# Two transformer blocks in one kernel: the second block's modulations moved beside the first feed-forward, background work queued behind fixed instructions of VectorE, state-space tables cut into small steps

## The chip, the cores and the metric

The kernel runs on one core of one Trainium2 chip, as one launch. The metric is the device time of a launch in microseconds; before the change it is 2636.41 us, the median of three runs (2634.53, 2636.41 and 2639.88).

## What is computed

512 tokens of width 1024 go through two blocks; 256 context tokens go with them through the first half of block 1. Cut to what matters here:

```
# block 1 (x: 512 tokens, h: 256 context tokens; c, c_ctx: one vector each)
ml = silu(c) @ ada_w + ada_b          # 9 vectors of 1024: shifts, scales, gates
mc = silu(c_ctx) @ ada_w + ada_b      # the first 5 of them are used
x = x + 0.5*ml[2] * swiglu(rms(x)*(1+ml[1])+ml[0])     # ffn1, x and h
h = h + 0.5*mc[2] * swiglu(rms(h)*(1+mc[1])+mc[0])
x = x + ml[5] * token_mix(...)                          # mLSTM and HGRN scans
x = x + 0.5*ml[8] * swiglu(rms(x)*(1+ml[7])+ml[6])      # ffn2
x = rms(x)                                              # final norm
# block 2
sh1, sc1, gt1, sh2, sc2, gt2 = split(silu(c_2) @ w_ada + b_ada, 6)
x = x + gt1 * mix(rms(x)*(1+sc1)+sh1)                   # attention and S5 state-space mixer
x = x + gt2 * conv_swiglu(rms(x)*(1+sc2)+sh2)           # up, causal conv, down
```

The S5 mixer needs tables (powers of a complex decay times its input and output matrices, a rotation table and a short kernel) that depend on weights alone.

## The kernel before, in words

**Matmuls.** Activations lie with features on partitions and tokens on the free axis. Each float32 weight tile (128x1024) is loaded into `wraw` (L195), copied into a rounded half `whi` by ScalarE (L203), and VectorE writes the rest `wlo` (L204); `mm3` (L208 to L218) makes a product of three passes, `whi*xh` (L215), `whi*xl` (L216) and `wlo*xh` (L218). There are three buffers of each.

**A feed-forward** (`ffn`, L424) has 11 groups. `stage_in` makes two hidden tiles of a group: PSUM tiles `psa` and `psu` (and `psc` for the context tokens), SiLU on ScalarE, a product `sa` (L438) and its split `hh`, `hl` (L441, L442). `stage_out` of the group before adds the down projection: eight tiles `pso`, from two banks, which VectorE adds to the residual `xr` (L491) or, for the context, `hr` (L494). The first hidden tile of a feed-forward is done in two halves of 256 tokens (L464 to L468), as its input is normalised half by half: `ssq_rstd` (L367) squares and sums the residual, takes a root on ScalarE (L374), a reciprocal on VectorE (`col`, L375), and spreads the result over partitions by four matmuls (L363) into `rs`; `norm_tile` then makes eight tiles `nt`, `xmh`, `xml` (L401 to L408) by VectorE, ScalarE and GpSimd.

**Modulations.** Those of ffn1's own input are made ahead of it (`ffn1_start`). The others come from `ada_steps` (L286): the rows of the modulation matrix come in tiles of 1 MB (`araw`, L293, two buffers, SyncE's queue), and VectorE multiplies each of their two halves with the broadcast vector `crow` (its SiLU is L283) and sums, by one SCALAR_TENSOR_TENSOR with an accumulator each (L305). Block 1 has 28 such tiles and 80 accumulations, and they are the background of ffn1. Block 2 has 24 tiles and 48 accumulations, and they are the background of ffn2, ahead of the S5 tables (`s5_tables`, L1383 on): some 200 short VectorE instructions, twelve GpSimd ones of 2048 columns (`big4`, L1509), 40 transposes and 64 small matmuls.

**Order.** The background is a Python generator. `tick()` (L322) runs it to its next `yield`, and is called twice after each hidden tile and once after every four output tiles. A tick decides only where instructions stand in the program text: a list scheduler then orders each engine's queue by that place and by when it takes an operand to be ready, so background work that is ready early is issued early. What the background still has to do is emitted before group 10 (`drain`).

Of the kernel before, what the change touches and what calls it, by code (L numbers as in the profile page):

```python
# [8 lines left out]
F32 = mybir.dt.float32  # L9
# [5 lines left out]
ALU = mybir.AluOpType  # L15
# [127 lines left out]
class Net:  # L143
# [142 lines left out]
    def ada_steps(self, src, bias, ids, jobs, done=None):  # L286


        nc = self.nc
        cr = self.c_rows(ids)  # L290
        todo = [(c, b0 + b, b, outs) for c, b0, outs in jobs for b in range(4)]

        def load(i):  # L293
            if i < len(todo):
                w = self.adp.tile([128, 2, D], F32, tag="araw", name=self.nm("araw"), bufs=2)
                nc.sync.dma_start(w, src[todo[i][1]])
                return w
        w = load(0)
        for i, (c, _, b, outs) in enumerate(todo):
            nxt = load(i + 1)  # L300
            for n, o in enumerate(outs):
                for h in range(2):
                    k = 2 * b + h
                    junk = self.adp.tile([128, D], BF16, tag="ajunk", name=self.nm("ajunk"), bufs=1)
                    nc.vector.scalar_tensor_tensor(junk, w[:, h], 1.0, cr[:, n], ALU.mult, ALU.mult,  # L305
                                                   accum_out=o[:, k : k + 1])
                yield
            if b == 3:
                for o in outs:
# [9 lines left out]
        yield  # L319
        self.tc.cur_priority -= n  # L320

    def tick(self):  # L322
        if self.bg is not None:
            next(self.bg, None)

    def drain(self):
        for _ in self.bg or ():
# [96 lines left out]
    def ffn(self, segs, w_in, w_out, act=None, group0=None, tail=None, nlast=2):  # L424
# [6 lines left out]
        def act_in(j, ps, hs):  # L431
            for si, (xm, wd, _, _) in enumerate(segs):
                if act is not None:
                    sa = act(ps[si][0], ps[si][1], j)
                else:
                    sa = self.tp.tile([128, T], F32, tag="sq", name=self.nm("sa"), bufs=4)[:, :wd]
                    nc.scalar.activation(sa, ps[si][0], AF.Silu)
                    nc.vector.tensor_tensor(sa, sa, ps[si][1], ALU.mult)  # L438
                hh = self.hhp.tile([128, wd], F32R, tag=f"hh{si}", name=self.nm("hh"), bufs=6)
                hl = self.hhp.tile([128, wd], F32R, tag=f"hl{si}", name=self.nm("hl"), bufs=6)  # L440
                nc.scalar.activation(hh, sa, AF.Copy)  # L441
                nc.vector.tensor_tensor(hl, sa, hh.bitcast(F32), ALU.subtract)  # L442
                hs[si].append((hh, hl))

        def stage_in(gi):
            hs = [[] for _ in segs]
            for jj, j in enumerate((gi * 2, gi * 2 + 1)):
                if gi == 0 and group0 is not None:
                    act_in(j, group0[jj], hs)
                    self.tick()  # L450
                    self.tick()
                    continue
                ww = [self.weights(w_in[2 * j + ai], [KT, 128]) for ai in range(2)]
                ws = [[(wh[:, k], wl[:, k]) for k in range(KT)] for wh, wl in ww]
# [17 lines left out]
                        for si, (xm, wd, _, _) in enumerate(segs):  # L472
                            self.mm3(ps[si][ai], ws[ai], xm)
                act_in(j, ps, hs)
                self.tick()
                self.tick()
            return hs

        def stage_out(gi, hs):
            ww = [self.weights(w_out[gi * 2 + jj], [D]) for jj in range(2)]  # L480
            w = lambda n: [(wh[:, n * 128 : n * 128 + 128], wl[:, n * 128 : n * 128 + 128]) for wh, wl in ww]
            for n2 in range(0, KT, 2):
                for si, (_, wd, res, gt) in enumerate(segs):
                    po = None
                    for n in (n2, n2 + 1):
                        if wd == T or n == n2:
                            po = self.bank("o", [128, 2, 256] if wd < T else [128, 512])
                        p = po if wd == T else po[:, n - n2]
                        self.mm3(p, w(n), hs[si])
                        if wd == T:  # L490
                            nc.vector.scalar_tensor_tensor(res[n], p, gt[:, n : n + 1], res[n], ALU.mult, ALU.add)  # L491
                    if wd < T:
                        for n in (n2, n2 + 1):
                            nc.vector.scalar_tensor_tensor(res[n], po[:, n - n2], gt[:, n : n + 1], res[n],  # L494
                                                           ALU.mult, ALU.add)
                if n2 % 4 == 2:
                    self.tick()

        def finish(gi, hs):

# [15 lines left out]
        for gi in range(NG):  # L516
            if gi == NG - 1:
                self.drain()
            hs.append(stage_in(gi))
            if gi == 1:  # L520
                self.tick()
                self.tick()
# [14 lines left out]
    def block1_ffn1(self):  # L537
        nc, tc = self.nc, self.tc
        with ExitStack() as es:
# [772 lines left out]
    def block1_ffn2(self):  # L1312
        nc, tc = self.nc, self.tc
        with ExitStack() as es:
            pool = lambda **k: es.enter_context(self.pool(**k))
            self.kinds = dict(u="a", s="p", o="t")
            self.tp, self.hhp = pool(name="tmp", bufs=2, side="right"), pool(name="hid", bufs=6)
            self.adp = self.bgs.enter_context(self.pool(name="ada", bufs=2, side="right"))
# [3 lines left out]
            jobs = [(c, 4 * c, (self.mod2[:, c],)) for c in range(6)]  # L1322
# [60 lines left out]
    def s5_tables(self, w, tag):  # L1383
# [19 lines left out]
        nc.scalar.activation(r8, mag, AF.Exp, scale=8.0)  # L1403
        nc.scalar.activation(mag, mag, AF.Exp)
        TT(th, li, step, mult)
        big = 1.5 * 2.0 ** 23
        nc.vector.tensor_scalar(n, th, 1.0 / (2 * np.pi), big, mult, add)
        nc.vector.tensor_scalar(n, n, big, None, sub)
        for c in (6.28125, 0.00193500518798828125, 3.0199159819567e-7):
            nc.vector.scalar_tensor_tensor(th, n, -c, th, mult, add)  # L1410
        lim = 3.1415925
        nc.vector.tensor_scalar(th, th, lim, -lim, ALU.min, ALU.max)
        u_re, u_im, ab = sm(), sm(), sm()
# [20 lines left out]
        at = lambda k: (P[0][:, :, k], P[1][:, :, k])  # L1434
        for k in range(2, 9):
            cmul(at(k), at(k // 2), at(k - k // 2))

        nre, den, fre, fim = sm(), sm(), sm(), sm()
        nc.vector.tensor_scalar(nre, P[0][:, :, 1], 1.0, None, sub)
# [5 lines left out]
        TT(t2, P[1][:, :, 1], li, mult)  # L1445
        TT(fre, t1, t2, add)
        TT(fre, fre, den, mult)
        TT(t1, P[1][:, :, 1], lr, mult)
        TT(t2, nre, li, mult)
        TT(fim, t1, t2, sub)  # L1450
# [12 lines left out]
        for o, (x, y), op in ((BB[0], (0, 1), sub), (BB[1], (1, 0), add)):  # L1463
            TT(o, bcw[:, x], c3(fre), mult)
            TT(tb, bcw[:, y], c3(fim), mult)
            TT(o, o, tb, op)

        U = [(u_re, u_im)]
        for _ in range(3):
            o = (sm(), sm())  # L1470
            cmul(o, U[-1], U[-1])
            U.append(o)
        rot = [sm((N, G, 64), tag="s5r") for _ in range(2)]
        nc.vector.memset(rot[0][:, :, 0], 1.0)
        nc.vector.memset(rot[1][:, :, 0], 0.0)
# [3 lines left out]
        while m < 64:  # L1479
# [4 lines left out]
            TT(hi[0], lo[0], b_[0], mult)  # L1484
            TT(t, lo[1], b_[1], mult)
            TT(hi[0], hi[0], t, sub)
            TT(hi[1], lo[0], b_[1], mult)
            TT(t, lo[1], b_[0], mult)
            TT(hi[1], hi[1], t, add)
            m *= 2  # L1490
            if m < 64:
                o = (sm(), sm())
                cmul(o, pw, pw)
                pw = o
        dt = lambda shape, nm: self.dp.tile(shape, F32, name=nm)
        self.s5d = dict(rot=dt([2, N, G, 64], "s5rot"), r8=dt([N, G], "s5r8"), bin=dt([2, N, G, N], "s5bin"),
                        out=dt([2, N, G, N], "s5out"), m=dt([N, 8, 512], "s5m"))
# [9 lines left out]
        yield  # L1507

        def big4(x, y, part, s0, s1):  # L1509
            o = w.tile([N, G, 8, 16], F32, tag="s5b", name=self.nm("s5b"), bufs=2)  # L1510
            t = w.tile([N, G, 8, 16], F32, tag="s5b", name=self.nm("s5b"), bufs=2)
            if part == 0:
                gp(o, x[0], y[0], mult)
                gp(t, x[1], y[1], mult)
                gp(o, o, t, s0)
            else:
                gp(o, x[0], y[1], mult)
                gp(t, x[1], y[0], mult)
                gp(o, o, t, s1)
            return o  # L1520
        krow, ksum = [sm((N, 8, N), tag="s5r") for _ in range(2)]
        for part in range(2):
            W1 = big4(pin, b4, part, sub, add)
            for q4 in range(4):
                pt = self.bank(tag, [N, 4, N])
                for x in range(4):
                    nc.tensor.transpose(pt[:, x], W1[:, q4 * 4 + x].rearrange("p t c -> p (t c)"), self.ident)
# [26 lines left out]
            if r < N:  # L1554
                nc.gpsimd.dma_start(self.s5d["m"][r:, t], zt[r:])
        for part in range(2):
            o = big4(pout, c4, part, add, sub)
# [511 lines left out]
```

## Time and profile before

| | |
|---|---|
| median of three runs | 2636.41 us |
| profiled execution, its time | 2634.42 us |
| its span, first to last instruction | 2632.6 us |
| TensorE matmuls busy | 2524.9 us, 96% |
| VectorE busy | 1653.0 us, 63% |
| ScalarE busy | 964.1 us, 37% |
| GpSimd busy | 458.8 us, 17% |
| mean granted TensorE clock | 0.977 |

The profile is of one execution, whose time is 1.8 us more than its span. A matmul that is issued late but overlaps the one before still counts as busy, so the 96% says less than the count of matmuls in a stretch does. In time the stages are: start to 80 us, ffn1 to some 570, the mix of block 1 to 1540, ffn2 to 1925, the mix of block 2 to some 2270, the last feed-forward to the end.

### The profile page before, as it was taken

What the parts mean: (1) busy time and instruction counts of PE and PEld (TensorE: products, weight loads), DVE (VectorE), ACT (ScalarE), POOL (GpSimd) and SP (SyncE); (2) the same over time, 40 slices, a digit from 0 to 9 for tenths busy, and PEclk for the clock granted to TensorE, in tenths of its full rate; (3) what the DMA queues carried; (4) which work ended last, traced back from release to release, by engine and by line L of the source; (5) the groups of instructions that cost most, each with busy time, mean ns of one, the idle gap of its engine ahead of it and who ended that gap; (6) DMA issues with size and microseconds to landing.
All of it is one profiled execution on the core that took longest, in us unless ns stands there. A gap on an engine that the chain in (4) does not pass through costs nothing. (4 is left out here: it accounts for less than half of the span.)

```text
span 2632.6 us, 38056 instructions
## 1 busy us (share of the span) xinstructions
PE 2524.9 (96%) x15116; PEld 2159.4 (82%) x15116; DVE 1653.0 (63%) x3071; ACT 964.1 (37%) x1710; POOL 458.8 (17%) x547
## 2 busy tenths in 40 slices
PE   6999999999989998999999988999999999999998
PEld 4888888899978888897888886788886768888887
DVE  8897534446499995425433489964565677766665
ACT  5311212236323332416422362222343466633333
POOL 3000000012044334314000012250012350100001
PEclk8999999999999999999999998999999899999999
DMA  6557211222211111111333376653414223333332
GB/s 228 178 193 252 91 55 57 81 72 79 71 49 41 49 33 41 37 56 50 103 111 92 118 228 224 218 179 98 151 41 147 57 64 102 120 96 96 96 96 73
DMA packets 88307, 277.94 MB, mean 106 GB/s; under 512 B 12912, under 2 KB 31104, under 8 KB 79936
## 3 DMA queue, kind: packets, MB, share of 16 engines
q1 hardware_dynamic: 85344, 265.00, 31.3%
q0 software_dynamic: 2064, 7.35, 0.8%
q10 hardware_dynamic: 720, 3.15, 0.3%
q8 instruction: 119, 1.95, 0.3%
q14 instruction: 60, 0.49, 0.1%
HBM read 262.88 MB, written 12.59 MB: 105 GB/s over the span
## 5 line engine op out<-in xcount | busy, mean ns | idle before, releaser
L204 DVE TENSOR_TENSOR wlo<-wraw,whi 128x1024 fp32r<-128x1024 f32 (+1 forms) x341 | 426.6, 1257 | 268.0 <-ACT whi L203 132.9
L203 ACT ACTIVATE whi<-wraw 128x1024 fp32r<-128x1024 f32 (+1 forms) x341 | 355.1, 1053 | 562.8 <-PE psp L216 157.2
L215 PE MATMUL psp<-xmh,whi 128*128 128x512 f32 (+1 forms) x760 | 283.6, 379 | 3.5 <-ACT K L807 3.1
L216 PE MATMUL psp<-xml,whi 128*128 128x512 f32 (+1 forms) x744 | 275.8, 377 | 0.0
L347 POOL TENSOR_TENSOR ssum<-ssum,sq 128x256 f32<-128x256 f32 x40 | 30.2, 755 | 1012.8 <-ACT sq L345 1012.4
L216 PE MATMUL psa<-xml,whi 128*128 128x512 f32 x496 | 194.7, 393 | 1.1 <-DVE xml L404 1.1
L215 PE MATMUL pso<-hh,whi 128*128 128x512 f32 (+1 forms) x512 | 185.7, 368 | 9.7 <-DVE xr L491 7.2
L215 PE MATMUL psa<-xmh,whi 128*128 128x512 f32 x496 | 194.9, 393 | 0.0
L216 PE MATMUL psu<-xml,whi 128*128 128x512 f32 x496 | 193.2, 390 | 0.0
L215 PE MATMUL psu<-xmh,whi 128*128 128x512 f32 x496 | 193.1, 389 | 0.0
L216 PE MATMUL pso<-hl,whi 128*128 128x512 f32 (+1 forms) x512 | 184.7, 366 | 0.0
L305 DVE SCALAR_TENSOR_TENSOR ajunk<-araw,crow 128x1024 bf16<-128x1024 f32 x128 | 160.6, 1254 | 25.9 <-DMA araw<-in_ada_r_dram 25.2
L215 PEld LDWEIGHTS psp<-xmh,whi 128*128 128x128 f32 x760 | 149.8, 197 | 28.8 <-ACT K L807 4.8
L218 PE MATMUL psp<-xmh,wlo 128*128 128x512 f32 (+1 forms) x744 | 172.2, 372 | 0.0
L216 PEld LDWEIGHTS psp<-xml,whi 128*128 128x128 f32 x744 | 146.8, 197 | 22.1 <-issue 0.6
L218 PEld LDWEIGHTS psp<-xmh,wlo 128*128 128x128 f32 x744 | 131.8, 193 | 26.3 <-issue 4.4
L218 PE MATMUL pso<-hh,wlo 128*128 128x512 f32 (+1 forms) x512 | 145.4, 365 | 3.4 <-DVE wlo L204 3.4
L491 DVE SCALAR_TENSOR_TENSOR xr<-pso,hgate,xr 128x512 f32<-128x512 f32 x128 | 94.9, 747 | 68.7 <-PE pso L218 68.6
L218 PE MATMUL psa<-xmh,wlo 128*128 128x512 f32 x496 | 126.4, 391 | 0.1
L218 PE MATMUL psu<-xmh,wlo 128*128 128x512 f32 x496 | 124.3, 390 | 1.3 <-DVE wlo L204 1.2
L441 ACT ACTIVATE hh<-sa 128x512 fp32r<-128x512 f32 x66 | 36.8, 562 | 241.9 <-DVE sa L438 241.7
L215 PEld LDWEIGHTS pso<-hh,whi 128*128 128x128 f32 x512 | 97.1, 190 | 27.3 <-DVE xr L491 5.8
(670 smaller groups left out, 5812.4 us busy)
## 6 DMA issues: line engine op xcount, KB each, us to landing
araw<-in_ada_r_dram SPq DMA_DIRECT2D x52, 1024.0 KB, 5.8
wraw<-in_ffn_in_dram SPq DMA_DIRECT2D x88, 512.0 KB, 3.9
wraw<-in_mix_fm_dram SPq DMA_DIRECT2D x65, 512.0 KB, 3.7
wraw<-in_ffn_out_dram SPq DMA_DIRECT2D x44, 512.0 KB, 3.7
wraw<-in_up_dram SPq DMA_DIRECT2D x44, 512.0 KB, 3.7
wraw<-in_down_dram SPq DMA_DIRECT2D x22, 512.0 KB, 3.7
araw<-in_ada_w_dram SPq DMA_DIRECT2D x8, 1024.0 KB, 11.8
wraw<-in_mix_out_dram SPq DMA_DIRECT2D x14, 512.0 KB, 3.7
```

What stands on the lines that cost most here:

```text
L203: nc.scalar.activation(hi, raw, AF.Copy)
L204: nc.vector.tensor_tensor(lo, raw, hi.bitcast(F32), ALU.subtract)
L215: self.nc.tensor.matmul(ps, wh, xh, start=k == 0, stop=False)
L216: self.nc.tensor.matmul(ps, *((wl, xh) if last else (wh, xl)), start=False, stop=False)
L218: self.nc.tensor.matmul(ps, *((wh, xl) if last else (wl, xh)), start=False, stop=k == n - 1)
L305: nc.vector.scalar_tensor_tensor(junk, w[:, h], 1.0, cr[:, n], ALU.mult, ALU.mult, accum_out=o[:, k : k + 1])
L347: (eng or nc.vector).tensor_tensor(acc, acc, t, ALU.add)
L441: nc.scalar.activation(hh, sa, AF.Copy)
L491: nc.vector.scalar_tensor_tensor(res[n], p, gt[:, n : n + 1], res[n], ALU.mult, ALU.add)
```

## The change

1. All 52 modulation tiles are now the background of ffn1, block 1's first and then block 2's; ffn2 keeps the S5 tables alone. The generator yields after every accumulation instead of after every two.
2. `tick(n)` runs the generator `n` times, inside `issue_after(anchor)`: every VectorE instruction that it emits gets an edge, for order in the queue only, behind the anchor. The anchor is the last `hl` of a hidden tile or the last residual addition of a `stage_out`. Ticks run 4 steps after a hidden tile and 3 after four output tiles in ffn1, and 2 and 1 in ffn2.
3. `s5_tables` yields after each short group of instructions. `big4` becomes `quarter`, called 16 times: of its three instructions, each now on 512 columns, the second product moves from GpSimd to VectorE.

```diff
@@ ada_steps
                     nc.vector.scalar_tensor_tensor(junk, w[:, h], 1.0, cr[:, n], ALU.mult, ALU.mult,
                                                    accum_out=o[:, k : k + 1])
-                yield
+                    yield
@@
-    def tick(self):
+    def tick(self, n=1):
         if self.bg is not None:
-            next(self.bg, None)
+            with self.tc.issue_after(self.anchor.ins):
+                for _ in range(n):
+                    next(self.bg, None)
@@ act_in
-                nc.vector.tensor_tensor(hl, sa, hh.bitcast(F32), ALU.subtract)
+                self.anchor = nc.vector.tensor_tensor(hl, sa, hh.bitcast(F32), ALU.subtract)
@@ stage_in
-                self.tick()
-                self.tick()
+                self.tick(self.pace[0])
@@ stage_out
-                            nc.vector.scalar_tensor_tensor(res[n], p, gt[:, n : n + 1], res[n], ALU.mult, ALU.add)
+                            self.anchor = nc.vector.scalar_tensor_tensor(res[n], p, gt[:, n : n + 1], res[n],
+                                                                         ALU.mult, ALU.add)
...
                 if n2 % 4 == 2:
-                    self.tick()
+                    self.tick(self.pace[1])
@@ block1_ffn1
-            self.bg = self.ada_steps(self.ins["ada_r"], "ada_b", (0, 1), jobs, done)
+            jobs2 = [(c, 4 * c, (self.mod2[:, c],)) for c in range(6)]
+
+            def bg():
+                yield from self.ada_steps(self.ins["ada_r"], "ada_b", (0, 1), jobs, done)
+                yield from self.ada_steps(self.ins["ada_r2"], "ada_b2", (2,), jobs2)
+            self.bg, self.pace = bg(), (4, 3)
@@ block1_ffn2
-            def bg():
-                yield from self.ada_steps(self.ins["ada_r2"], "ada_b2", (2,), jobs)
-                yield from self.s5_tables(s5p, "s")
-            self.bg = bg()
+            self.bg, self.pace = self.s5_tables(s5p, "s"), (2, 1)
@@ s5_tables (one yield at the start of the tables becomes some 40)
-        def big4(x, y, part, s0, s1):
-            o = w.tile([N, G, 8, 16], F32, tag="s5b", name=self.nm("s5b"), bufs=2)
-            t = w.tile([N, G, 8, 16], F32, tag="s5b", name=self.nm("s5b"), bufs=2)
-            if part == 0:
-                gp(o, x[0], y[0], mult)
-                gp(t, x[1], y[1], mult)
-                gp(o, o, t, s0)
...
+        def quarter(o, x, y, part, s0, s1, q4):
+            gs = slice(4 * q4, 4 * q4 + 4)
+            t = w.tile([N, 4, 8, 16], F32, tag="s5q", name=self.nm("s5q"), bufs=2)
+            gp(o[:, gs], x[0][:, gs], y[part][:, gs], mult)
+            TT(t, x[1][:, gs], y[1 - part][:, gs], mult)
+            gp(o[:, gs], o[:, gs], t, (s0, s1)[part])
```

Three places of the queues. The first is ScalarE's at the entry of ffn2, between the squares of the second half (`sq`) and the root that the second half's normalisation waits for (`col`). `s5s` are small tables, `crow` the broadcast vector of block 2. Before:

```order
L1400 ACTIVATE s5s_14930<-vec 128x16
L345 ACTIVATE sq_13814<-xr_13222 128x256
L1403 ACTIVATE s5s_14936<-s5s_14931 128x16
L1404 ACTIVATE s5s_14931<-s5s_14931 128x16
L1416 ACTIVATE s5s_14948<-s5s_14932 128x16
L1417 ACT_TABLE_LOAD
L1417 ACTIVATE s5s_14947<-s5s_14932 128x16
L283 ACT_TABLE_LOAD
L283 ACTIVATE crow_13997<-crow_13997 128x1024
L1418 ACTIVATE s5s_14946<-s5s_14948,s5s_14949 128x16
L374 ACT_TABLE_LOAD
L374 ACTIVATE col_13820<-psp_13817,epsc 128x2
```

and in the changed kernel:

```order
L1400 ACT_TABLE_LOAD
L1400 ACTIVATE s5s_14147<-vec 128x16
L348 ACTIVATE sq_13967<-xr_13375 128x256
L377 ACT_TABLE_LOAD
L377 ACTIVATE col_13973<-psp_13970,epsc 128x2
```

Eight instructions between the square and the root, two of them table loads, are gone from there.

The second is VectorE's queue in the same place, where the eight tiles of the second half are normalised. Before, with accumulations (L305) and table steps between the tiles:

```order
L406 SCALAR_TENSOR_TENSOR nt_13835<-xr_13222,ga_13224,rs_13227 128x256
L305 SCALAR_TENSOR_TENSOR ajunk_14004,mod_87<-araw_14000,crow_13997 128x1024
L1430 TENSOR_TENSOR s5s_14954<-s5s_14960,s5s_14961 128x16
L408 SCALAR_TENSOR_TENSOR xml_92<-nt_13826,modx,xmh_91 128x256
L408 SCALAR_TENSOR_TENSOR xml_92<-nt_13835,modx,xmh_91 128x256
L305 SCALAR_TENSOR_TENSOR ajunk_14006,mod_87<-araw_14000,crow_13997 128x1024
L1431 TENSOR_TENSOR s5s_14960<-s5s_14954,s5s_14955 128x16
L1432 TENSOR_TENSOR s5s_14961<-s5s_14955,s5s_14954 128x16
L404 TENSOR_TENSOR xml_92<-nt_13830,xmh_91 128x256
```

and now:

```order
L409 SCALAR_TENSOR_TENSOR nt_13988<-xr_13375,ga_13377,rs_13380 128x256
L411 SCALAR_TENSOR_TENSOR xml_92<-nt_13979,modx,xmh_91 128x256
L411 SCALAR_TENSOR_TENSOR xml_92<-nt_13988,modx,xmh_91 128x256
L407 TENSOR_TENSOR xml_92<-nt_13983,xmh_91 128x256
L409 SCALAR_TENSOR_TENSOR nt_13997<-xr_13375,ga_13377,rs_13380 128x256
```

Nothing stands between the tiles any more.

The third is VectorE's queue in a group of ffn1, between residual additions (L491 and L494 before, L492 and L496 now). Before, in its second `stage_out`:

```order
L491 SCALAR_TENSOR_TENSOR xr<-pso_1509,hgate_734,xr 128x512
L305 SCALAR_TENSOR_TENSOR ajunk_1770,modc<-araw_1565,crow_749 128x1024
L442 TENSOR_TENSOR hl_1476<-sa_1472,hh_1475 128x256
L305 SCALAR_TENSOR_TENSOR ajunk_1899,modx<-araw_1762,crow_749 128x1024
L305 SCALAR_TENSOR_TENSOR ajunk_1901,modx<-araw_1762,crow_749 128x1024
L305 SCALAR_TENSOR_TENSOR ajunk_1903,modc<-araw_1762,crow_749 128x1024
L494 SCALAR_TENSOR_TENSOR hr_113<-pso_1517,hgate_734,hr_113 128x256 x2
```

and now, in its fourth:

```order
L492 SCALAR_TENSOR_TENSOR xr<-pso_2362,hgate_734,xr 128x512
L305 SCALAR_TENSOR_TENSOR ajunk_2334,modx<-araw_2198,crow_749 128x1024
L305 SCALAR_TENSOR_TENSOR ajunk_2338,modx<-araw_2330,crow_749 128x1024
L305 SCALAR_TENSOR_TENSOR ajunk_2340,modx<-araw_2330,crow_749 128x1024
L496 SCALAR_TENSOR_TENSOR hr_113<-pso_2370,hgate_734,hr_113 128x256 x2
```

Runs of three to four accumulations ahead of a residual addition were there before and are there now; the accumulations go on to the ninth group instead of ending near the fourth.

## Rows read from the trace of the kernel before

**Rows 1.** The page, its first line.
```profile
span 2632.6 us, 38056 instructions
```
**Rows 2.** Stretches: start:end and length; busy us and instructions by engine, clock, DMA share, GB/s.
```profile
132.00:198.00 66.00, 66.00 (x383) 58.37 (x382) 61.95 (x108) 12.80 (x18) 0.00 (x0) 1.00 0.57 196
198.00:264.00 66.00, 61.91 (x347) 53.65 (x347) 52.11 (x90) 11.31 (x18) 0.00 (x0) 1.00 0.72 250
...
2376.00:2442.00 66.00, 66.00 (x292) 54.64 (x292) 41.50 (x52) 24.05 (x29) 0.00 (x0) 1.00 0.30 96
```
**Rows 3.** What TensorE waited for, 1535 to 1730 us: total, times, longest.
```profile
PE pso L215 <- DVE xr L491: 5.6, 2, 3.3
PE psp L363 <- DVE col L375: 3.8, 1, 3.8
PE pso L218 <- DVE wlo L204: 3.4, 3, 2.1
PE psa L464 <- ACT xmh L407: 2.6, 2, 2.1
...
PE psa L216 <- DVE xml L404: 1.1, 1, 1.1
```
**Rows 4.** ScalarE in order of time at the entry of ffn2: start, us, what.
```profile
1538.83 1.28 ACT L1417 ACT_TABLE_LOAD   x1
...
1540.35 1.28 ACT L283 ACT_TABLE_LOAD   x1
1541.65 1.06 ACT L283 ACTIVATE crow<-crow 128x1024 f32<-128x1024 f32 x1
...
1542.92 1.28 ACT L374 ACT_TABLE_LOAD   x1
```
**Rows 5.** TensorE in order of time, same place.
```profile
1540.65 0.28 PE L468 MATMUL psu<-xml,whi 128*128 128x256 f32 x1
1544.73 1.22 PE L363 MATMUL psp<-ident,col 128*128 128x128 f32 x4 [3.80 <-DVE col L375]
```
**Rows 6.** VectorE in order of time, same place.
```profile
1547.78 1.21 DVE L305 SCALAR_TENSOR_TENSOR ajunk<-araw,crow 128x1024 bf16<-128x1024 f32 x1
...
1552.41 1.75 DVE L305 SCALAR_TENSOR_TENSOR ajunk<-araw,crow 128x1024 bf16<-128x1024 f32 x1
```
**Rows 7.** VectorE alone in that stretch: busy us, instructions, clock, DMA.
```profile
1546.30:1558.30 12.00, 11.90 (x29) 0.70 0.65 147
```
**Rows 8.** Stretches of ffn2, columns as in rows 2.
```profile
1543.30:1553.20 9.90, 6.37 (x24) 5.82 (x25) 8.02 (x23) 4.87 (x11) 2.54 (x3) 0.50 0.74 180
1620.00:1645.00 25.00, 16.18 (x53) 11.49 (x52) 25.00 (x28) 2.62 (x4) 14.20 (x4) 0.73 0.39 129
1720.00:1770.00 50.00, 50.00 (x283) 41.37 (x282) 30.47 (x23) 14.27 (x19) 34.58 (x26) 1.00 0.54 186
```
**Rows 9.** VectorE in order of time in ffn2.
```profile
1599.57 0.68 DVE L442 TENSOR_TENSOR hl<-sa,hh 128x512 fp32r<-128x512 f32 x1
...
1629.33 3.82 DVE L1430 TENSOR_TENSOR s5s<-s5s,s5s 128x16 f32<-128x16 f32 x1
```
**Rows 10.** GpSimd in order of time in ffn2.
```profile
1627.72 5.39 POOL L1515 TENSOR_TENSOR s5b<-s5b,s5b 128x2048 f32<-128x2048 f32 x1
1633.19 3.69 POOL L1517 TENSOR_TENSOR s5b<-s5s,s5s 128x2048 f32<-128x2048 f32 x1
```
**Rows 11.** GpSimd on 256 columns, a group of the page: busy, mean ns, idle before.
```profile
L347 POOL TENSOR_TENSOR ssum<-ssum,sq 128x256 f32<-128x256 f32 x40 | 30.2, 755 | 1012.8 <-ACT sq L345 1012.4
```
**Rows 12.** What TensorE waited for, 66 to 560 us (ffn1).
```profile
PE pso L215 <- DVE hr L494: 2.3, 1, 2.3
PE pso L215 <- DVE xr L491: 1.6, 1, 1.6
```
**Rows 13.** The accumulations of ffn1: ns min/median/max, first and last start; idle time before them.
```profile
L305 DVE SCALAR_TENSOR_TENSOR ajunk<-araw,crow x80: 1209/1218/1229, 88.7 to 274.1; 128x1024 bf16<-128x1024 f32 x80
...
  DMA araw<-in_ada_r_dram: 17.4, 6
```

More of the change, by code (lines that the diff above doesn't have):

```diff
@@ L474, in stage_in @@
                 act_in(j, ps, hs)
-                self.tick()
-                self.tick()
+                self.tick(self.pace[0])
             return hs
@@ L490, in stage_out @@
                         if wd == T:
-                            nc.vector.scalar_tensor_tensor(res[n], p, gt[:, n : n + 1], res[n], ALU.mult, ALU.add)
+                            self.anchor = nc.vector.scalar_tensor_tensor(res[n], p, gt[:, n : n + 1], res[n],
+                                                                         ALU.mult, ALU.add)
                     if wd < T:
                         for n in (n2, n2 + 1):
-                            nc.vector.scalar_tensor_tensor(res[n], po[:, n - n2], gt[:, n : n + 1], res[n],
-                                                           ALU.mult, ALU.add)
+                            self.anchor = nc.vector.scalar_tensor_tensor(res[n], po[:, n - n2], gt[:, n : n + 1], res[n],
+                                                                         ALU.mult, ALU.add)
                 if n2 % 4 == 2:
-                    self.tick()
+                    self.tick(self.pace[1])
         def finish(gi, hs):
@@ L520, in ffn @@
             if gi == 1:
-                self.tick()
-                self.tick()
+                self.tick(2)
             if 0 < gi <= NG - nlast:
@@ L1317, in block1_ffn2 @@
             self.tp, self.hhp = pool(name="tmp", bufs=2, side="right"), pool(name="hid", bufs=6)
-            self.adp = self.bgs.enter_context(self.pool(name="ada", bufs=2, side="right"))
             s5p = self.bgs.enter_context(self.pool(name="s5t", bufs=1, side="right"))
@@ L1321, in block1_ffn2 @@
             nc.vector.tensor_scalar(hx, self.modx[:, 8], 0.5, None, ALU.mult)
-            jobs = [(c, 4 * c, (self.mod2[:, c],)) for c in range(6)]
-            def bg():
-                yield from self.ada_steps(self.ins["ada_r2"], "ada_b2", (2,), jobs)
-                yield from self.s5_tables(s5p, "s")
-            self.bg = bg()
+            self.bg, self.pace = self.s5_tables(s5p, "s"), (2, 1)
             st = [None, None]
@@ L1405, in s5_tables @@
         TT(th, li, step, mult)
+        yield
         big = 1.5 * 2.0 ** 23
@@ L1410, in s5_tables @@
             nc.vector.scalar_tensor_tensor(th, n, -c, th, mult, add)
+        yield
         lim = 3.1415925
@@ L1436, in s5_tables @@
             cmul(at(k), at(k // 2), at(k - k // 2))
+            yield
         nre, den, fre, fim = sm(), sm(), sm(), sm()
@@ L1447, in s5_tables @@
         TT(fre, fre, den, mult)
+        yield
         TT(t1, P[1][:, :, 1], lr, mult)
@@ L1466, in s5_tables @@
             TT(o, o, tb, op)
+            yield
         U = [(u_re, u_im)]
@@ L1472, in s5_tables @@
             U.append(o)
+            yield
         rot = [sm((N, G, 64), tag="s5r") for _ in range(2)]
@@ L1486, in s5_tables @@
             TT(hi[0], hi[0], t, sub)
+            yield
             TT(hi[1], lo[0], b_[1], mult)
@@ L1494, in s5_tables @@
                 pw = o
+            yield
         dt = lambda shape, nm: self.dp.tile(shape, F32, name=nm)
@@ L1506, in s5_tables @@
         gp = nc.gpsimd.tensor_tensor
-        yield
-        def big4(x, y, part, s0, s1):
-            o = w.tile([N, G, 8, 16], F32, tag="s5b", name=self.nm("s5b"), bufs=2)
-            t = w.tile([N, G, 8, 16], F32, tag="s5b", name=self.nm("s5b"), bufs=2)
-            if part == 0:
-                gp(o, x[0], y[0], mult)
-                gp(t, x[1], y[1], mult)
-                gp(o, o, t, s0)
[L1516 to L1520, printed above, removed]
+        def quarter(o, x, y, part, s0, s1, q4):
[4 more added lines that the diff above has]
+            gp(o[:, gs], o[:, gs], t, (s0, s1)[part])
+        big = lambda: w.tile([N, G, 8, 16], F32, tag="s5b", name=self.nm("s5b"), bufs=2)
         krow, ksum = [sm((N, 8, N), tag="s5r") for _ in range(2)]
         for part in range(2):
-            W1 = big4(pin, b4, part, sub, add)
+            W1 = big()
             for q4 in range(4):
+                quarter(W1, pin, b4, part, sub, add, q4)
+                yield
                 pt = self.bank(tag, [N, 4, N])
@@ L1556, in s5_tables @@
         for part in range(2):
-            o = big4(pout, c4, part, add, sub)
+            o = big()
+            for q4 in range(4):
+                quarter(o, pout, c4, part, add, sub, q4)
+                yield
             nc.gpsimd.dma_start(self.s5d["out"][part], o.rearrange("p g t c -> p g (t c)"))
```

## The prediction

> **What bounds the kernel now.** I read the views in this order: the page's shares, the windows by stage, TensorE's waits, then single stretches in order of time. The page gives the profiled execution a span of 2632.6 us [rows 1]; its time is 2634.4, which is 2.0 below the median of the three runs. TensorE bounds nearly all of it. At full clock with no wait, a stretch of 66 us holds 292 matmuls of 512 columns [rows 2], or 0.226 us for one. In ffn2, 50 us hold 283 matmuls, TensorE is busy for 50.00 and nothing is waited for [rows 8]. There a change to another engine is worth nothing. So the question is where TensorE falls below that rate beside the work that the change moves, and there are three such places.
>
> *The entry of ffn2.* TensorE ends its first-half work at about 1540.9 and then waits 3.80 us for `col` [rows 5]. The root that makes `col` stands on ScalarE behind three table loads of 1.28 us and the SiLU of `crow` of 1.06 us [rows 4]; the last of the loads belongs to the root itself, the others to the tables and to `crow`. Then come the eight tiles of the second half: VectorE is busy for 11.90 of 12.0 us [rows 7], accumulations of 1.21 to 1.75 us stand between the tiles [rows 6], TensorE waits 2.6 us on `xmh` and 1.1 on `xml` [rows 3], and its granted clock is 0.50, the level of 1.2 GHz, for 9.9 us in which it is busy for only 6.37 [rows 8].
>
> *The middle of ffn2.* From 1620 to 1645, VectorE is busy for 25.00 of 25.00 us and TensorE issues 53 matmuls, at a mean clock of 0.73 [rows 8]. At 0.226 us each those are 12.0 us of work, so 13.0 are lost. Two of the waits are for the residual `xr`, 5.6 us together, and the longest of three for `wlo` is 2.1 [rows 3]. The reason stands in the lines of VectorE and GpSimd: a GpSimd instruction of 2048 columns runs from 1627.72 for 5.39 us [rows 10], and a VectorE one of 16 columns that begins at 1629.33 takes 3.82, until that same end [rows 9]. Its length is the remainder of GpSimd's. VectorE is held off while it has accumulations to do as well, and falls behind.
>
> *ffn1.* 80 accumulations of 1.22 us run from 88.7 to 274.1 [rows 13]. Over the whole of ffn1 TensorE waits for the residuals only 2.3 and 1.6 us [rows 12], both in the stretch where the tiles come fastest (250 GB/s, 347 matmuls in 66 us against 383 in the stretch before it, which has TensorE at 66.00 of 66.00 with VectorE at 61.95 [rows 2]).
>
> **The change part by part.**
>
> *Entry (term A).* The eight ScalarE instructions between square and root go. The root then meets its ones-matmuls at about the time when TensorE ends its own work, so the 3.8 us go whole; the root keeps one table load. Four accumulations stood between the tiles, two of 1.21 and two of 1.75 (the first and the third of them in [rows 6]), 5.9 us in all. VectorE was the engine waited for, so its time is TensorE's, but ScalarE and GpSimd make a share of each tile: I take two thirds, 4.0. A = 7.8. The lower bound is 3.8 (the tiles bound by ScalarE anyway), the upper 9.7 (all of the 5.9).
>
> *Middle (term B).* 48 accumulations leave ffn2, 48 x 1.22 = 59 us of VectorE [rows 13]. What comes to VectorE is 16 multiplications of 512 columns, near the `hl` subtraction of that size at 0.68 [rows 9]: 11 us. On GpSimd 12 instructions of at least 3.69 us [rows 10] become 32 of 512 columns. None of that size is in the trace; between 0.755 at 256 columns [rows 11] and 3.69 at 2048 a straight line gives 1.17, so 32 of them take 38 us against 44. A hold is then at most about 1.2 us instead of 5. The loss that can come back is the 13.0 us, and 1.3 us of the other two waits for `wlo`, later in ffn2 [rows 3]: 14.3. I leave three holds of 1.17 in place, 3.5 us. B = 10.8. The upper bound is 14.3; the lower is 5.6, the two waits for `xr` alone.
>
> *The rest of ffn2.* The table steps now have places of their own, at most 2 behind a hidden tile and 1 behind four output tiles. VectorE has 30.47 of 50 us in a group there with its GpSimd beside it at 34.58 and TensorE waits for nothing [rows 8], so I cost this at 0, with a loss of up to 2 us as its bound. The steps are 43 and there are 6 places' worth in a group, so they end by the eighth group and nothing is left for the drain.
>
> *ffn1 (term C).* 128 accumulations instead of 80. The steps are 4 + 4 behind the hidden tiles and 3 + 3 between outputs, 14 in a group of some 50 us, or 17 us of VectorE; before, 80 in 187 us were 21 in 50 us. The rate of block 2's tiles is 7 in a group, as two accumulations use up one; before, 28 in 187 us were 7.5 in 50. So neither VectorE nor the queue of SyncE gets more in a group than it had; the load lasts to about the ninth group, 530 us, instead of to 274. VectorE's own work is less from the end of the context's share on. The cover of the accumulations is VectorE's idle time, which was 4.05 of 66 us in the dense stretch with no loss [rows 2]. C = 0. What it could gain is the 3.9 us of the two waits [rows 12]; what it could lose is bounded by two such waits more and one of 2.3 for the longer stretch, 6 us. The accumulations are pinned behind an anchor, so they cannot run early when VectorE is idle, and a residual addition behind them in the queue waits for their tile too: that is the second rival below.
>
> *Sum.* 7.8 + 10.8 + 0 + 0 = 18.6 us. 2634.4 - 18.6 = 2615.8, and 2617.8 with the 2.0 us that the median of the runs stands above this execution. **I predict 2618 us.** With all lower bounds it is 3.8 + 5.6 - 6 - 2 = 1.4 us (2635); with all upper, 9.7 + 14.3 + 3.9 = 27.9 (2608.5).
>
> **The rivals.**
>
> *1. The pieces keep holding VectorE off.* The row shows that a VectorE instruction waits for the whole rest of a GpSimd one [rows 9, 10]. The change gives VectorE 16 more instructions with both inputs in SBUF beside 32 GpSimd ones, and the two alternate by data: a GpSimd product, VectorE's, and a sum of both. If VectorE's additions to the residual stay late through that, only the two waits on `xr` go: B = 5.6, and 2636.4 - 7.8 - 5.6 = 2623.0. For it: GpSimd's total stays near 38 us. Against it: with 34.58 of 50 us on GpSimd, TensorE lost nothing when VectorE had no accumulations [rows 8]. The Trainium skill, "SBUF — State Buffer", section "Who interferes with whom", says that a VectorE instruction with two SBUF inputs contends with a GpSimd one that reads SBUF, and that one of the two is blocked and not merely slowed; by that rule, which the 3.82 us bears out, the move of a product to VectorE speaks against the change.
>
> *2. Slower: pinned accumulations wait for `araw` at the head of VectorE's queue.* Before, VectorE sat idle 6 times, 17.4 us in all, for `araw` [rows 13], which is 2.9 us each. Such an accumulation blocks the residual addition behind it, which frees the bank that the next `pso` needs. In the change there are two such places in a group, between output tiles, over nine groups: 18. If each costs the 2.3 us of the longer wait seen [rows 12], ffn1 loses 41 us against 3.9 before, 37 more: 2617.8 + 37 = 2655. The change is slower by over 0.2% from 13 places on (29.9 - 3.9 - 18.6 = 7.4 us). For it: with two buffers a tile can be asked for only when the accumulation two tiles before is done, and the accumulations come in bursts of 3 or 4. Against it: in the order of before there were such runs too, and only 2 of them cost anything.
>
> *3. The middle's waits are not the accumulations'.* If GpSimd's holding made the whole loss of 1620 to 1645, and the finer pieces only spread it, A alone is left: 2636.4 - 7.8 = 2628.6.
>
> *4. It does not do what it says.* The edge could be without effect, or TensorE's order could be bound elsewhere in ffn2, so that the waits appear a tile later: 2636.4.
>
> **How the numbers follow.** The forecast has 0.58, rival 1 0.17, rival 2 0.10, rival 3 0.08 and rival 4 0.07. The range reaches from the upper bounds, 2608, past rivals 1 and 3 to 2632; outside it are rivals 2 and 4 and a little of the forecast. A measurement of this kernel can tell about 0.2%, 5.3 us, from no change, which puts the border of faster at 2631.1. Forecast, rival 1 and rival 3 are below it but for their tails (0.05 together): faster 0.78. Same is rival 4 with these tails, 0.12. Slower is rival 2, 0.10.
>
> **What would show it.** Right: at the entry no wait on `col` of over 1 us, the root on ScalarE right behind the squares, a granted clock of 1.00 within two or three us; in ffn2's middle no wait for `xr` of over 1 us, and VectorE below 0.8 in every stretch of 25 us; GpSimd pieces of 1.0 to 1.4 us; in ffn1 no more than 4 us of waits for `pso` and the accumulations spread until some 530 us. The prediction would be wrong if `pso` waits on `xr` or `hr` turn up in most groups of ffn1 with VectorE idle on `araw` beside them (rival 2), if the clock of 0.50 comes back later in ffn2 (rivals 1 and 3), or if TensorE's entry wait only changes its name from `col` to `xmh`.

## The result, and the profile after

The changed kernel takes 2607.1 us (median of four, 2605.3 to 2609.5) against 2635.7 for the one before beside it: a ratio of 0.9889, 95% interval 0.9872 to 0.9906. Faster, as forecast, but by 28.6 us in place of 18.6, and 0.9 us below the lower end of the range.

The page's first line, against [rows 1]:

```profile
span 2605.4 us, 38102 instructions
```

The span is 27.2 us shorter. To see where, I compare the starts of the same TensorE instruction, found by its tiles and its place among them, in the two traces. One such pair stands behind the entry of ffn2 and one near its end. In the trace of before:

```profile
1571.22 0.39 PE L215 MATMUL psa<-xmh,whi 128*128 128x512 f32 x1
...
1899.92 0.39 PE L216 MATMUL psu<-xml,whi 128*128 128x512 f32 x1
```

and in that of the changed kernel:

```profile
1562.48 0.39 PE L215 MATMUL psa<-xmh,whi 128*128 128x512 f32 x1
...
1870.98 0.39 PE L216 MATMUL psu<-xml,whi 128*128 128x512 f32 x1
```

From 8.74 us early to 28.94: this stage alone gains 20.2. The same for all stages, bounded by the starts at 84, 560, 1528, 1571, 1900 and 2320 us of before (minus is a gain; each row is one profiled execution). The last 25 us of ffn2, from 1900 us on, are in the column of mix 2. "Pins" are the edges behind anchors:

| kernel | to 84 | ffn1 | mix 1 | entry of ffn2 | rest of ffn2 | mix 2 | sum |
|---|---|---|---|---|---|---|---|
| changed | -0.8 | -1.8 | +1.4 | -7.5 | -20.2 | +1.7 | -27.2 |
| e13, changed again | +2.2 | +0.4 | +1.5 | -7.5 | -20.2 | +4.4 | -19.3 |
| e1, move alone | 0.0 | +8.4 | -1.1 | -4.4 | -5.7 | +0.9 | -2.0 |
| e2, places alone | -0.1 | -5.4 | +0.2 | -4.3 | -15.9 | +10.0 | -15.5 |
| e3, no pins | +0.1 | +2.3 | +1.8 | -4.1 | -3.5 | +2.1 | -1.2 |
| e7, pins in ffn1 only | 0.0 | -1.8 | +0.7 | -3.2 | -5.2 | +2.1 | -7.3 |
| e8, pins in ffn2 only | -0.3 | +3.9 | -0.3 | -7.5 | -20.2 | +1.8 | -22.7 |
| e11, coarse steps, pinned | -0.7 | -3.4 | +2.1 | -7.6 | -4.5 | +2.3 | -11.7 |
| e4, pieces of 2048 | +0.7 | -1.3 | +1.7 | -7.4 | -12.5 | +4.2 | -14.6 |
| e5, product on GpSimd | -0.9 | +0.5 | +0.4 | -8.9 | -14.2 | +2.2 | -20.9 |
| e9, small matmuls apart | 0.0 | 0.0 | +0.9 | -7.5 | -18.3 | +3.3 | -21.6 |
| e6, one stream | -0.3 | -5.3 | +0.8 | -7.4 | -20.2 | +5.2 | -27.3 |
| e12, one stream again | 0.0 | -5.3 | 0.0 | -7.7 | -20.2 | -0.2 | -33.3 |

The start and the two mixes move by some us between executions of one kernel (changed and e13, e6 and e12), and ffn1 of the changed kernel by 2.2; the two ffn2 columns of these pairs repeat within 0.3. So what follows is read by stage.

ScalarE at the entry of ffn2, against [rows 4]: the root is behind its own table load, and nothing is behind it.

```profile
1535.26 0.40 ACT L348 ACTIVATE sq<-xr 128x256 f32<-128x256 f32 x1
1535.68 1.28 ACT L377 ACT_TABLE_LOAD   x1
1538.61 0.26 ACT L377 ACTIVATE col<-psp,epsc 128x2 f32<-128x2 f32 x1 [1.64 <-PE psp L356]
```

TensorE's waits from 1535 to 1730 us, against [rows 3]; one is left of six groups:

```profile
PE psa L466 <- ACT xmh L410: 2.1, 1, 2.1
```

Stretches of ffn2, against [rows 8] (columns as there; the engines are TensorE, its weight loads, VectorE, ScalarE and GpSimd): the entry, the third and fourth group, and the one with most of the tables' matmuls.

```profile
1536.30:1546.20 9.90, 7.80 (x50) 7.00 (x49) 5.03 (x10) 5.46 (x12) 2.64 (x4) 0.84 0.60 116
1591.00:1616.00 25.00, 25.00 (x112) 20.67 (x112) 19.79 (x40) 7.04 (x8) 9.29 (x8) 1.00 0.34 103
1686.00:1736.00 50.00, 50.00 (x298) 40.94 (x297) 27.80 (x32) 16.03 (x22) 22.38 (x21) 1.00 0.38 123
```

TensorE is full again with VectorE at 0.8 and below, and GpSimd runs its pieces beside it. In ffn1 the accumulations and the one wait for `pso` that is left, against [rows 13] and [rows 12]:

```profile
L305 DVE SCALAR_TENSOR_TENSOR ajunk<-araw,crow x128: 1211/1222/1228, 95.1 to 528.8; 128x1024 bf16<-128x1024 f32 x128
...
  DMA araw<-in_ada_r_dram: 19.6, 8
```

```profile
PE pso L215 <- DVE hr L496: 1.8, 1, 1.8
```

### The profile page after: what moved, and what is told of

It reads as the page before. It is cut to its first block, busy times and chain, and to the rows that moved or that the text cites. A ratio compares the mean times of both kernels' runs of the same rounds, so it can differ in the third digit from the quotient of the medians.

```text
span 2605.4 us, 38102 instructions
## 1 busy us (share of the span) xinstructions
PE 2512.9 (96%) x15116; PEld 2157.3 (83%) x15116; DVE 1651.4 (63%) x3087; ACT 965.1 (37%) x1711; POOL 452.2 (17%) x567
## 5 line engine op out<-in xcount | busy, mean ns | idle before, releaser
L305 DVE SCALAR_TENSOR_TENSOR ajunk<-araw,crow 128x1024 bf16<-128x1024 f32 x128 | 156.4, 1222 | 25.2 <-DMA araw<-in_ada_r_dram 19.6
L492 DVE SCALAR_TENSOR_TENSOR xr<-pso,hgate,xr 128x512 f32<-128x512 f32 x128 | 95.3, 749 | 109.8 <-PE pso L218 109.7
## 6 DMA issues: line engine op xcount, KB each, us to landing
araw<-in_ada_w_dram SPq DMA_DIRECT2D x8, 1024.0 KB, 11.7
```

The costliest lines, as they stand in the source:

```text
L492: self.anchor = nc.vector.scalar_tensor_tensor(res[n], p, gt[:, n : n + 1], res[n], ALU.mult, ALU.add)
```

## The experiments

### Is it the load or the place? (e1, e2, e3)

Two theories for the 20 us: VectorE has 59 us less to do in ffn2 (the prediction's term B), or nothing of the background stands ahead of what TensorE waits for. e1 is the kernel before with the move alone:

```diff
-            self.bg = self.ada_steps(self.ins["ada_r"], "ada_b", (0, 1), jobs, done)
+            jobs2 = [(c, 4 * c, (self.mod2[:, c],)) for c in range(6)]
+
+            def bg():
+                yield from self.ada_steps(self.ins["ada_r"], "ada_b", (0, 1), jobs, done)
+                yield from self.ada_steps(self.ins["ada_r2"], "ada_b2", (2,), jobs2)
+            self.bg = bg()
@@ block1_ffn2
...
-            self.bg = bg()
+            self.bg = self.s5_tables(s5p, "s")
```

> The kernel before with one part of the change: block 2's modulation tiles moved into ffn1. Ticks, the scheduler's free choice of place and the tables with GpSimd instructions of 2048 columns stay as before. Theory 1 (the load did it: VectorE had too much work in ffn2, and 59 us of it are gone): the whole 20 us in the middle of ffn2 come back; at the entry the table loads of the Sin stay ahead of the root, so 2 to 3 of the 7.5 us there are lost again; about 2611 us. Theory 2 (the place did it: table steps and accumulations hoisted in front of what TensorE waits for): half of the middle or less comes back, since the tables are still bunched: 2618 to 2626 us, with waits of TensorE on xr or wlo of over 1 us in ffn2.

2632.8 us, ratio 0.9987 (0.9974 to 1.0001): nothing that can be told from no change, and slower than both theories had it. Only 5.7 of the 20 us in ffn2 come, though no accumulation is left there. VectorE is still full, with table steps, while TensorE gets through 24 matmuls, of some 44 at 0.226 us each (e1, columns as in [rows 8]):

```profile
1590.00:1600.00 10.00, 4.89 (x24) 3.73 (x22) 9.83 (x56) 2.62 (x5) 0.00 (x0) 0.97 0.21 62
```

They stand ahead of the product `sa`. ScalarE waits for `sa`, and its copy `s5e`, which stands behind that in its queue and which TensorE waits for, is late as well (ScalarE, then TensorE of e1):

```profile
1597.38 0.63 ACT L441 ACTIVATE hh<-sa 128x512 fp32r<-128x512 f32 x1 [13.23 <-DVE sa L438]
```

```profile
1599.98 1.97 PE L1526 MATMUL pss<-ident,s5b 128*128 128x128 f32 x8 [5.11 <-ACT s5e L1528]
```

And ffn1 loses 8.4. TensorE's waits for `pso` in ffn1 of e1:

```profile
PE pso L215 <- DVE hr L494: 6.0, 3, 3.5
PE pso L215 <- DVE xr L491: 3.0, 3, 1.3
```

The longest of them is this accumulation, free to go ahead of `hl` and of the residual of the context, waiting for its tile (VectorE of e1):

```profile
310.44 1.22 DVE L305 SCALAR_TENSOR_TENSOR ajunk<-araw,crow 128x1024 bf16<-128x1024 f32 x1 [3.43 <-DMA araw<-in_ada_r_dram]
...
311.59 0.69 DVE L442 TENSOR_TENSOR hl<-sa,hh 128x512 fp32r<-128x512 f32 x1
312.20 0.87 DVE L494 SCALAR_TENSOR_TENSOR hr<-pso,hgate,hr 128x256 f32<-128x256 f32 x2
```

That is rival 2's mechanism, and it is the version *without* pins that has it. e2 is the mirror image, the changed kernel with block 2's tiles back in ffn2, `self.pace = (3, 2)` there:

> The changed kernel with block 2's modulation tiles back in ffn2 (3 steps behind a hidden tile and 2 between outputs there), so pinned places and small table steps without the move. Theory 1 (load): TensorE still waits in the middle of ffn2, 10 us or more of the 20 are lost again, and the entry pays the SiLU of crow and its table load (2.3 us): 2618 to 2624 us. Theory 2 (place): VectorE's work in ffn2 is as much as before, but none of it stands ahead of what is waited for; the middle loses under 3 us, the entry 2 to 3: 2609 to 2612 us.

2620.0 us, ratio 0.9926 (0.9910 to 0.9942). The total lies in theory 1's range and not in theory 2's, but the stages do not go by theory 1: with all 48 accumulations in ffn2, its rest still gains 15.9 of the 20.2. From 1553 to 1800 us, which takes in all 48 (the last starts at 1710), TensorE waits for nothing. A stretch of e2 in that time (columns as in [rows 8]):

```profile
1650.00:1700.00 50.00, 50.00 (x222) 41.39 (x222) 40.73 (x63) 11.65 (x14) 0.00 (x0) 1.00 0.75 264
```

The 4.3 us are lost behind 1800 us, where the tables' matmuls now stand: TensorE waits 3.0 us there for ScalarE's copy `s5e` and 1.4 for `xr`. The tables end at 1868 us in place of 1786, and of the 10.0 in the column of mix 2 some 3.6 are lost before ffn2 ends, where TensorE waits 2.0 us for `whi`. So the load has a price too, some 8 us in ffn2, all of it where the tables come late. What the mix itself loses beyond that stays open.

e3 is the changed kernel with the edge taken out:

```diff
-            with self.tc.issue_after(self.anchor.ins):
-                for _ in range(n):
-                    next(self.bg, None)
+            for _ in range(n):
+                next(self.bg, None)
```

> The changed kernel without the edges behind anchors: move, small steps and pieces of 512 columns stay, the scheduler chooses places freely. Theory 1 (load): as the first run, about 2611 us. Theory 2 (place): the entry loses 2 to 3 us, the middle of ffn2 5 to 10 us: 2615 to 2620 us. In ffn1 the accumulations should end about the seventh group, in place of the ninth, with 4 us of waits in the fast stretch as before.

2633.1 us, ratio 0.9982 (0.9970 to 0.9994): without the pins the change is worth 4 us. It is worse than both theories had it. So the greater part of the 20 us is the place: the move without pins and small steps (e1) keeps 5.7 of them, and pins and small steps without the move (e2) keep 15.9.

### Which stage pays for which pins (e7, e8)

The same line, under `if self.pace == (4, 3)` or its opposite.

> The changed kernel, with the edges behind anchors in ffn1 and without them in ffn2 (the table steps there go where the scheduler puts them). If the pins in ffn2 make the gain there: ffn1 as in the changed kernel, the entry of ffn2 loses 3.5 us of its 7.5, the middle 16 to 17 us of its 20: 2625 to 2629 us. If the losses without pins came from accumulations of ffn1 alone: 2608 to 2612 us.

> The mirror image: edges behind anchors in ffn2 alone, the 128 accumulations of ffn1 free. If each stage pays for its own pins: ffn2 as in the changed kernel, and ffn1 loses 4 us (as the run without any pins, 2.3 us over before against 1.8 under it): 2610 to 2612 us. With the run before this one the two losses should add up to that of the run without any pins, 26 us over the changed kernel.

2626.7 us (ratio 0.9952, 0.9936 to 0.9968) and 2615.0 (0.9919, 0.9902 to 0.9936). Against the changed kernel's first profile e7 loses 19.4 us in ffn2 and e8 5.7 in ffn1, 25.1 together; e3 loses 24.3 in both. Each stage pays for its own. (In ffn1 e8 loses more than the 4 us it was put at, and its total is 3 us above what was expected.) e7 shows the mechanism at the entry, on ScalarE: with the tables free, the Sin and its table load stand ahead of the root again.

```profile
1537.52 1.28 ACT L1423 ACT_TABLE_LOAD   x1
...
1539.25 1.28 ACT L381 ACT_TABLE_LOAD   x1
1540.54 0.26 ACT L381 ACTIVATE col<-psp,epsc 128x2 f32<-128x2 f32 x1
```

And in the middle, on VectorE and then GpSimd of e7:

```profile
1587.70 1.27 DVE L1439 TENSOR_TENSOR s5s<-s5s,s5s 128x16 f32<-128x16 f32 x1
1589.01 1.24 DVE L1495 TENSOR_TENSOR s5s<-s5s,s5s 128x64 f32<-128x64 f32 x1
...
1591.29 1.21 DVE L204 TENSOR_TENSOR wlo<-wraw,whi 128x1024 fp32r<-128x1024 f32 x1
```

```profile
1586.65 3.51 POOL L1526 TENSOR_TENSOR s5b<-s5b,s5q 128x512 f32<-128x512 f32 x2 [2.17 <-DVE s5q L1525]
```

Instructions of 16 and 64 columns take 1.2 us while GpSimd works, `wlo` comes behind them, and TensorE pays (e7):

```profile
1592.56 0.80 PE L218 MATMUL pso<-hh,wlo 128*128 128x512 f32 x1 [4.38 <-DVE wlo L204]
1593.15 0.63 PE L215 MATMUL pso<-hh,whi 128*128 128x512 f32 x1
```

The second row is at the level of 1.2 GHz (granted clock 0.50 from 1593 to 1595 us), 0.63 us where it has 0.39 at 1.00: the clock has fallen behind the wait, so this wait costs more than its length. None of this needs an accumulation.

### Are the small steps needed? (e11)

The changed kernel without the new `yield`s ahead of the pieces, and one `yield` in their place; the pins stay.

> The changed kernel with the tables' short VectorE instructions in one step, as before the change, but behind an anchor. Theory A (the pin alone does it: nothing of the tables can stand ahead of what TensorE waits for at that point): the middle of ffn2 as in the changed kernel within 2 us, 2605 to 2610 us. Theory B (it takes small steps as well: some hundred short instructions behind one anchor hold VectorE's queue for over 20 us, and weights and residual additions behind them come late): 5 to 12 of the 20 us in the middle are lost again, 2612 to 2619 us, with waits of TensorE on wlo or xr in the first group of ffn2.

2623.6 us, ratio 0.9954 (0.9939 to 0.9968). Theory B, and more than it said: 15.7 of the 20.2 us are lost. TensorE's waits in ffn2 of e11:

```profile
PE pso L215 <- DVE xr L492: 7.1, 5, 3.3
PE pso L218 <- DVE wlo L204: 2.7, 1, 2.7
...
```

A pin behind an anchor says what goes first, not how much follows. With one long step, it all stands behind one hidden tile and ahead of the next group's work.

### The pieces and their product (e4, e5, e9)

e4 has the twelve GpSimd instructions of 2048 columns again (`big4`), pinned:

> The changed kernel with the twelve GpSimd instructions of 2048 columns in place of the pieces of 512 and the products on VectorE; pins and move stay. If long holds of VectorE by GpSimd were what made the loss (rival 3 of the prediction turned round): VectorE instructions of 3 to 5 us come back and TensorE waits again, 2614 to 2620 us. If a hold costs only where VectorE has accumulations to do as well: within 2 us of the changed kernel, 2605 to 2609 us, with VectorE instructions of 3 to 5 us that nobody waits for.

2617.0 us, ratio 0.9920 (0.9905 to 0.9935); 7.7 of the 20.2 us are lost. Long holds do cost without accumulations, so rival 3 had a part of it. GpSimd and VectorE of e4:

```profile
1611.60 3.71 POOL L1521 TENSOR_TENSOR s5b<-s5s,s5s 128x2048 f32<-128x2048 f32 x1 [8.95 <-DVE s5s L1470]
1615.38 4.61 POOL L1522 TENSOR_TENSOR s5b<-s5b,s5b 128x2048 f32<-128x2048 f32 x1
```

```profile
1611.66 3.68 DVE L1435 TENSOR_TENSOR s5s<-s5s,s5s 128x16 f32<-128x16 f32 x1
...
1615.46 4.56 DVE L1431 TENSOR_TENSOR s5s<-s5s 128x16 f32<-128x16 f32 x1
1619.95 1.21 DVE L204 TENSOR_TENSOR wlo<-wraw,whi 128x1024 fp32r<-128x1024 f32 x1
```

Each short one lasts until GpSimd's ends, and `wlo` is late by both; TensorE's only waits in that stage are for `wlo`, 2.4 and 0.3. That is not 7.7. The rest shows in e5, where the second product goes back to GpSimd, in pieces (`gp` for `TT` in `quarter`):

> The changed kernel with the second product of each piece back on GpSimd: 48 GpSimd instructions of 512 columns, none of the 16 multiplications on VectorE. By the page's rule on the shared reads (rival 1), a product on VectorE beside GpSimd's pieces costs holds, so this version should be the faster one, by up to some 3 us, or equal if VectorE has slack: 2604 to 2607 us. If the pieces' place counts instead (GpSimd's chain for a piece is a third longer, so the small matmuls that wait for it come later): equal or up to 5 us slower, 2607 to 2612 us.

2614.8 us, ratio 0.9915 (0.9900 to 0.9929), slower than both theories had it: 6.0 us lost in that stage, though TensorE waits only 1.2. As e4 has the product on GpSimd too, the length of the pieces is left with the difference of the two, 1.7 of its 7.7. What differs in e5 is how the tables' 64 small matmuls lie, which the trace has as 128 records. By form in that stage, of e5, then of the changed kernel (us busy, mean ns):

```profile
L1542 PE MATMUL pss<-s5b,s5s 64*32 64x128 f32 x128 | 7.3, 276 | 0.0
```

```profile
L1542 PE MATMUL pss<-s5b,s5s 64*32 64x128 f32 x128 | 4.3, 271 | 0.0
```

and of before:

```profile
L1537 PE MATMUL pss<-s5b,s5s 64*32 64x128 f32 x128 | 6.5, 275 | 0.0
```

Where they come in three runs they take 4.3 us, in e5's 13 runs 7.3. e9 breaks up the runs by a `yield` behind every four:

> The changed kernel with a step of its own for every four of the tables' 64 small matmuls, so that TensorE does them in eight runs among the large ones in place of three. Theory (a run of small matmuls costs some 0.23 us besides its matmuls, and 0.1 us more at the large ones beside it: in the trace 4 records of them take 0.35 us, 12 take 0.56, 64 take 1.88): 5 more runs, 1.5 to 2 us more in the middle of ffn2 and nothing else. Rival (the order of the small matmuls costs nothing, and the 3 us more that they take where GpSimd makes the products is a wait on GpSimd): no change in that stage, within 0.3 us.

The runs are eight, and the stage loses 2.0 us, as worked out; the total is 2613.6 us against 2611.6 for the changed kernel beside it. By these 0.4 us for a run, e5's ten more runs are some 4 us (an estimate), which with its wait of 1.2 is most of the 6.0. It is not quite "nothing else": the added steps also bring half of the runs some 50 us later, the tables end at 1867 us, and another 1.7 us are lost in the last 25 us of ffn2. So the number of runs and their place are not wholly told apart.

### The one wait left in ffn1 (e6, e12, e13)

In the changed kernel, at the switch from block 1's tiles to block 2's (VectorE):

```profile
382.05 1.23 DVE L305 SCALAR_TENSOR_TENSOR ajunk<-araw,crow 128x1024 bf16<-128x1024 f32 x1 [3.53 <-DMA araw<-in_ada_r_dram]
...
384.46 0.87 DVE L496 SCALAR_TENSOR_TENSOR hr<-pso,hgate,hr 128x256 f32<-128x256 f32 x2
```

The second generator asks for `crow` and its first tile only when it is begun. e6 makes it one list of tiles with one `crow` of three vectors:

```diff
-        todo = [(c, b0 + b, b, outs) for c, b0, outs in jobs for b in range(4)]
+        todo = [(src, bias, n0, c, b0 + b, b, outs) for src, bias, n0, jobs in parts for c, b0, outs in jobs for b in range(4)]
...
-            self.bg, self.pace = bg(), (4, 3)
+            self.bg, self.pace = self.ada_steps((0, 1, 2), parts, done), (4, 3)
```

> The changed kernel with block 1's and block 2's tiles as one stream: the broadcast vector of block 2 is made at the start with the other two, and its first tile is asked for while the last of block 1 is at work. Theory (rival 2 happened at one place, the switch of the two streams at 382 us, where an accumulation at the head of VectorE's queue waits 3.5 us for its tile): the loss of 3.6 us there goes, ffn1 stands at 5.4 us below before as in the run with pins and without the move, and the total is 2603 to 2604 us. Rival: the wait goes on to another tile in the same group, as the queue of SyncE is what is late, and the total stays at 2607.

> The version with one stream of tiles once more, beside the changed kernel on the same chip. The stage of ffn1 should again stand 3.6 us under the changed kernel's; the total 1 to 4 us under it. If the gain is given back behind ffn1, in the mix of block 2, each time, the totals are equal.

> The changed kernel itself, as the measure for the runs beside it: 2605 to 2610 us, and in its trace the same stages as in the first profile: ffn1 2 us under before, the entry of ffn2 7.5, its middle 20, and a mix of block 2 that differs from run to run by a few us.

e6 takes 2605.0 us, ratio 0.9876 (0.9861 to 0.9891). e12 has 2602.6 (0.9870, 0.9852 to 0.9889), and the changed kernel beside it 2611.6 (0.9902, 0.9887 to 0.9917), above the 2605 to 2610 that it was put at. The `pso` wait is gone from ffn1 in both e6 and e12, whose ffn1 is 3.6 and 5.8 us shorter than in the changed kernel's two profiles; these have waits of 1.8 and 4.0 there. The medians are 2 us (e6, against the first runs of the changed kernel) and 9 us (e12) apart, and the intervals overlap. So the wait is shown gone and this version is the fastest measured, by an amount that the runs do not settle.

## Why the prediction was wrong

**Term A, right.** Forecast 7.8, measured 7.5 in both profiles. Its parts: e7, which has the Sin's load ahead of the root and no accumulation, keeps only 3.2 of it; e2, with the SiLU of `crow` there, 4.3. So about 3 to 4 us are the root's place on ScalarE, as put at 3.8. One of its signs did not come: the granted clock was to be 1.00 within two or three us, and it is 0.50 from 1544 to 1546 and 1.00 from 1548 us on, behind the wait of 2.1 us for `xmh`, which was there before and stays.

**Term B, the step that failed.** It put down the middle of ffn2 to VectorE's load and to long holds: "48 accumulations leave ffn2, 48 x 1.22 = 59 us", and hence 10.8 us, at most 14.3; the places of the table steps it had under the rest of ffn2, at 0. Measured were 20.2, and in the main by those places. The move alone gives 5.7 (e1), pins and small steps without the move 15.9 (e2), the move and small steps without pins 3.5 (e3). The load was the wrong quantity: VectorE was full for 25 us because a list scheduler had hoisted all that was ready, and it stays full without the accumulations (24.89 of 25 us in e7):

```profile
1585.00:1610.00 25.00, 19.80 (x80) 15.59 (x79) 24.89 (x61) 5.20 (x8) 11.03 (x7) 0.86 0.24 73
```

The size was off for two more reasons. "I leave three holds of 1.17 in place, 3.5 us" was not due: holds go on (a piece's two GpSimd instructions average 1.28 and 1.71 us, longer than put), yet TensorE waits for none of them. And the bound of 14.3 took in one stretch of 25 us and two waits behind it. It left out the small matmuls, which were broken into many runs, 6.5 us in place of 4.3, and what that cost the large ones beside them. (Three of the 53 matmuls that it counted in the stretch are small ones too, of 0.27 us, so the stretch had lost some 0.6 us more than 13.0.) That the change came out faster, as forecast, does not bear out term B: the move that it paid for is worth nothing that can be measured by itself, and beside the pins the some 8 us of e2.

**The rest of ffn2 at 0**: right for the groups behind the middle, where TensorE waits for nothing. **Term C, forecast 0**: -1.8 and +0.4 in two profiles, within its bounds, but as a sum of two things that were named apart: both waits of [rows 12] go, and one of rival 2's kind comes, at one place of 18.

**Rival 1** (products on VectorE held by GpSimd): the holds are there, as in [rows 9, 10]; but the version that spares VectorE the products (e5) is 6.0 us slower in the stage. The Trainium skill, "SBUF — State Buffer", section "Who interferes with whom", is borne out as to who blocks whom (3.68 us for 16 columns beside GpSimd's 3.71, in e4). But the placement with more instructions exposed to such holds was the faster one here. **Rival 2**: excluded for the pinned kernel; it is what the unpinned ones do. **Rivals 3 and 4** fall with the 20.2 us, 3 but for the part that e4 leaves it.

## What to carry to other kernels

Background work on a shared engine costs first by where it stands in the queue, and only then by how much of it there is: tie it behind the instruction that frees the engine awaited, and cut it small, since either alone (beside the move) kept only 3.5 (small steps) or 4.5 (pins) of 20 us here. How much there is shows where it puts off what comes behind it, some 8 us in e2. When a busy engine is read as overloaded, look first at what it did in that stretch that nobody waited for. Where two streams of loads follow each other, let the first one's prefetch reach into the second.

## What was not expected of the hardware

A run of small matmuls among large ones has a price besides its matmuls: from its start to the next large matmul, one of four records takes 0.34 us in the kernel before and one of 64 takes 1.88 in the changed kernel, which is some 0.026 us for a record and 0.24 for the run (an estimate, by a straight line). And in the changed kernel the switch of the streams, with a wait of 1.8 us for `pso` up to 385 us, cost 3.6 by e6, as the granted clock was 0.50 for a while behind it (TensorE busy for 3.00 of 3.00 us with 12 matmuls):

```profile
386.00:389.00 3.00, 3.00 (x12) 2.61 (x11) 1.88 (x2) 0.00 (x0) 0.00 (x0) 0.50 0.88 341
```
